# Moving the first gate's four tanh behind attention's last exponentials in a two-layer hybrid decoder

## The chip, the cores and the metric

The kernel runs on one core of one Trainium2 chip. The metric is the device time of one execution in microseconds (us). Five engines work side by side, each through its own list of instructions in order: TensorE (PE, with its weight loads as PEld), VectorE (DVE), ScalarE (ACT), GpSimd (POOL) and SyncE (SP), which here mostly issues loads. An instruction that needs another engine's result waits on a semaphore, and everything behind it on its engine waits too.

## The reference

The reference computes two layers on x of 512 tokens by 1024 features, in float32. Each layer does:

```
h = rmsnorm(x) ; z = h @ w_in       # q,k,v of attention, q,k,v,o,i,f of the mLSTM, gates g_a, g_m
att = sliding-window attention(q, k, v, sinks)      # 8 heads, 2 key heads, blocks of 128 queries
hm  = mLSTM in chunkwise form, per-head norm, times sigmoid(o)
mixed = sigmoid(g_a) * (att @ w_att_branch) + sigmoid(g_m) * (hm @ w_m_branch)
x = x + mixed @ w_out
x = x + relu(rmsnorm(x) @ w_ff1)^2 @ w_ff2
```

Attention's softmax is p = exp(s - m), divided by the sum of p and exp(sink - m). The sigmoid of a gate is computed as (1 + tanh(g / 2)) / 2. g_a and g_m have 1024 columns each, which the kernel works off in four groups of 512: gates 0 and 1 are g_a, gates 2 and 3 are g_m.

## The kernel before

Each float32 operand of a large product is split into a high and a low part in the reduced type fp32r, and a product is three matmuls into one PSUM buffer (high by high, high by low, low by high). The split of a weight chunk (`chunk`, L144 to L167) is one copy on ScalarE (`wh`, L166) and one subtraction on VectorE (`wl`, L167). Chunks come from memory through three landing buffers and are split into four pairs of `wh`, `wl`; a landing buffer is free for the next load when its `wl` is done.

`mixer` computes everything of a layer up to w_out. After the projections of attention's inputs, one long list of PE steps follows: the mLSTM's q and k (8 units of length), gate 0 (8), gate 1 (8), the first part of the mLSTM's v and o (2), and then the product of attention's output with w_att_branch. A unit of length is one chunk of 128 input features by 512 columns, 12 matmuls of 128x512. A gate's projection (`gate_steps`) gathers four PSUM buffers (`bank()`, five in all) over 8 chunks; then `ev` runs four times: VectorE multiplies each buffer by the norm's row into the tile `p` (L700) and so frees it, and at m == 3 ScalarE takes the tanh of all four tiles (L703).

Attention runs beside this list. `weave` takes the list and a second one, `side`, of (position, function) pairs, and calls each side function when the list has come to its position. There are 8 attention units, 4 query blocks by 2 key heads. Unit i's scores (`att_scores`, PE, then a copy on ScalarE, L604, and a masked copy on VectorE, L605) stand at 7 + 1.65 i, the softmax (`att_softmax`: maximum on VectorE, four exponentials L618 and one for the sink, L620, on ScalarE, division on VectorE) 1.25 later, the transposes of the probabilities on PE (`att_probs`, L52) and their split (L176, L177) 3.45 later, and the product with the values (`att_out`, PE, then L649 and L656 on ScalarE, L653 and L657 on VectorE) 5.65 later. Before each block, its queries and keys are transposed on PE and read out of PSUM by pairs of ScalarE and VectorE (`q_tr` L585 and L586, `k_tr` L563 to L566). All small products of attention (names `aux`) share three PSUM buffers.

What stands in an engine's list is decided when the kernel is built: a scheduler takes the calls in the order of `weave`, and orders each engine's instructions by the dependences, by its own estimates, and by priorities. `tc.high_priority()` lets an instruction go ahead of others that are ready, and `with tc.issue_after(i)` holds one back until instruction i has been placed. The evictions of a gate, `ev` with its tanh, run at high priority (`group_steps`, `finish`).

A ScalarE function needs its table loaded. The scheduler puts a table load ahead of the first function that the loaded table does not hold; attention's first exponentials run with the table that is loaded at the program's start (LN_EXP), and a load stands ahead of the first tanh of a layer.

The result of gate 0's tanh is read by VectorE in `a_steps(0, g0)`, after the product with w_att_branch, which begins at position 26 of the list.

Of the kernel before, what the change touches and what calls it, by code (L numbers as in the profile page):

```python
# [12 lines left out]
AF = mybir.ActivationFunctionType  # L13
# [20 lines left out]
def hybrid_kernel(ctx, tc, x, norm_mix, w_in, att_q_norm, att_k_norm, att_sinks, m_gate_bias,  # L34
# [3 lines left out]
    ve, sc, gp = nc.vector, nc.scalar, nc.gpsimd  # L38
# [34 lines left out]
    def slot(dt=F32, shape=(P, T)):  # L73
        return now["act"].tile(list(shape), dt, tag="a", name=nm("a"))
# [20 lines left out]
    def sm(shape, tag, bufs=None):  # L95
        return small.tile(list(shape), F32, tag=tag, name=nm(tag), bufs=bufs)
# [112 lines left out]
    def feat_steps(acts, srcs, evac):  # L209

        def mm(ps, c, w, a, first, last):
            mm3(ps, w[0][:, c], w[1][:, c], a[0], a[1], first, last)

        return group_steps(acts, srcs, evac, T, mm)
# [174 lines left out]
    def mixer(l, norm, late, order, phase):  # L389
# [9 lines left out]
        def wcols(c0, n):  # L399
            return lambda k: [W[k * P:(k + 1) * P, c0:c0 + n]]  # L400
# [150 lines left out]
        def k_vec(b):  # L551
            rope(kvi[:, b, 0:128].rearrange("p (h d) -> p h d", d=HD), b, HKV)

        def k_tr(b):

            ps = aux([P, P])
            pe.transpose(ps, kvi[:, b, 0:128], ident)
            for h in range(HKV):
                r = slice(64 * h, 64 * h + 64)
                o = slice(64 - 64 * h, 128 - 64 * h)  # L560
                c = slice((b + 1) * P, (b + 2) * P)
                g = gcols[1][r, l:l + 1]
                sc.activation(kTh[r, h, c], ps[r, :], AF.Copy, scale=g)  # L563
                sc.activation(kTh[o, h, c], ps[r, :], AF.Copy, scale=g)
                ve.scalar_tensor_tensor(kTl[r, h, c], ps[r, :], g, f32(kTh[r, h, c]), op0=ALU.mult, op1=ALU.subtract)
                ve.tensor_copy(kTl[o, h, c], f32(kTl[r, h, c]))  # L566

        def q_vec(b):
            rope(q_tok[b].rearrange("p (h d) -> p h d", d=HD), b, HQ)

        def q_tr(b):


            ps = aux()
            for j in range(4):
                pe.transpose(ps[:, j * P:(j + 1) * P], q_tok[b][:, j * P:(j + 1) * P], ident)
            for j in range(2):
                qT[b, j] = temp(F32R)
                t4 = qT[b, j].rearrange("p (i n t) -> p i n t", n=2, i=2)
                p4 = ps[:, 2 * j * P:2 * (j + 1) * P].rearrange("p (n t) -> p n t", n=2)  # L580
                for i in range(2):
                    r = slice(64 * i, 64 * i + 64)
                    o = slice(64 - 64 * i, 128 - 64 * i)
                    g = gcols[0][r, l:l + 1]
                    sc.activation(t4[r, i], p4[r], AF.Copy, scale=g)  # L585
                    ve.scalar_tensor_tensor(t4[o, i], p4[r], g, f32(t4[r, i]), op0=ALU.mult,  # L586
                                            op1=ALU.subtract)

        def att_scores(b, kv, hp):
# [14 lines left out]
                sc.activation(dst, p4[:, :, 0, :], AF.Copy)  # L604
            ve.copy_predicated(dst, tri_i.unsqueeze(1).to_broadcast([P, 2, P]), p4[:, :, 1, :])  # L605

        def att_softmax(b, kv):
            sp = sps[b, kv]
            s3 = sp.rearrange("p (h k) -> p h k", h=4)
            hs = slice(4 * kv, 4 * kv + 4)  # L610
            m = sm([P, 4], "m")
            ve.tensor_reduce(m, s3, axis=AX.X, op=ALU.max)
            ve.scalar_tensor_tensor(m, m, -1.0, nsinks[:, l, hs], op0=ALU.mult, op1=ALU.min)
            es = sm([P, 4], "es")
            ve.tensor_tensor(es, sinks[:, l, hs], m, op=ALU.add)
            den = sm([P, 4], "den")
            for i in range(4):
                sc.activation(s3[:, i, :], s3[:, i, :], AF.Exp, bias=m[:, i:i + 1],  # L618
                              accum_out=den[:, i:i + 1])
            sc.activation(es, es, AF.Exp)  # L620
            ve.tensor_tensor(den, den, es, op=ALU.add)
            ve.reciprocal(den, den)
            ve.tensor_tensor(s3, s3, den.unsqueeze(2).to_broadcast([P, 4, P]), op=ALU.mult)
# [69 lines left out]
        def gate_steps(g, last=False):  # L693


            sg = []

            def ev(m, ps):
                sg.append(wide[g][:, m, :] if g < 2 else slot())
                ve.tensor_tensor(sg[m], ps, row[0], op=ALU.mult)  # L700
                if m == 3:
                    for t in sg:
                        i = sc.activation(t, t, AF.Tanh, scale=0.5)  # L703
                    if last:
                        with tc.issue_after(i.ins):
                            sc.preload_act_table_set(LN_EXP)

            return sg, feat_steps(acts, wcols(C_G + 512 * g, 512), ev)
# [124 lines left out]
        def vo_steps(*ns):  # L833
# [4 lines left out]
        side = [(0, lambda: k_vec(0)), (0, lambda: q_vec(0)), (0, lambda: k_vec(1)), (0, lambda: q_vec(1)),  # L838
                (7 - 1.25, lambda: k_tr(0)), (7 - 1.75, lambda: q_tr(0))]
        for i, (b, kv) in enumerate(units):  # L840
            at = 7 + 1.65 * i
            side += [(at, lambda b=b, kv=kv: att_scores(b, kv, 0)),
                     (at + 1.25, lambda b=b, kv=kv: att_scores(b, kv, 1)),
                     (at + 1.25, lambda b=b, kv=kv: att_softmax(b, kv)),
                     (at + 3.45, lambda b=b, kv=kv: att_probs(b, kv)),
                     (at + 3.45 + 2.2, lambda b=b, kv=kv: att_out(b, kv))]
            if kv == 0 and b + 1 < NB:
                if b + 2 < NB:
                    side += [(at + 1, lambda b=b: k_vec(b + 2)), (at + 1, lambda b=b: q_vec(b + 2))]
                side += [(at + 2 * 1.65 - 1.75, lambda b=b: k_tr(b + 1)), (at + 2 * 1.65 - 2.15, lambda b=b: q_tr(b + 1))]  # L850
# [3 lines left out]
                                  (43.5, 1, 0), (45.0, 3, 0), (46.5, 1, 1), (48.0, 3, 1))]  # L854
        g0, s0 = gate_steps(0)
        g1, s1 = gate_steps(1)

        hm = q_tok
        hss = sm([P, NB, MH], "hss", 1)
# [129 lines left out]
        def sum_next(key, g):  # L989
            b = scratch["b"]  # L990
            with behind():
                ve.scalar_tensor_tensor(b, b, -1.0, wide[g][:, :, 0:H], op0=ALU.mult, op1=ALU.subtract)
            for p in range(2):
                of_chain(key, p)
# [34 lines left out]
        def ready_pair(n, p):  # L1029
            with behind():  # L1030
                h, lo = split(qa[0][:, 2 * p:2 * p + 2, :], get=boxed(n, 2 * p, 2))
            for k in range(2):
                wo[n, 2 * p + k] = h[:, k, :], lo[:, k, :]
            sum_a(p, 1, 1 if n == 5 else 0)

        def ready_w(n, k):
            raw = {3: qb, 7: qb, 2: qc}[n][k] if n in (3, 7, 2) else qa[0][:, k, :]
            if n == 2:
                get = boxed(n, k)
            elif n == 3:  # L1040
                get = lambda: temp(F32R)
            else:
                tags = iter(("wh", "wl"))

                def get():
                    t = next(tags)
                    return now["wsp"].tile([P, T], F32R, tag=t, name=nm(t))

            with behind():
                wo[n, k] = split(raw, get=get)  # L1050
            if n == 1 and k % 2:
                sum_a(k // 2, 0, 1)
            if n == 3:
                with tc.high_priority():
                    gp.dma_start(raw, of_out(0, 1, k)[:, 0, :], accum_op=ALU.add)
# [63 lines left out]
        for n in (1, 5, 6, 3, 7, 2):  # L1119
            fill += p_steps(n)  # L1120
        fill += p_steps(4, by_tokens)
        side = [(0.3, lambda: ready_w(1, 3)), (2.3, lambda: ready_pair(5, 0)), (4.3, lambda: ready_pair(5, 1)),
                (4.9, sum3), (6.2, lambda: ready_pair(6, 0)), (8.6, lambda: ready_pair(6, 1)),
                (10.3, lambda: sum_next("s2", 0)), (11.7, lambda: sum_next("s4", 1))]
# [505 lines left out]
    for l in range(DEPTH):  # L1630
        with start if l == 0 else ExitStack() as phase:
            if l > 0:
                psum_pools(phase, 3)
            norm = mixer(l, norm, late, order, phase)
        late = norm.steps(0, 1.5, 0.5)
        with ExitStack() as phase:
            psum_pools(phase, 2)
            norm = mlp(l, norm, late, phase)
        late = norm.steps(0, 1.5, 0.5, lambda k, norm=norm: turn_behind(norm, k)) if norm else []
        order = [4, 5, 6, 7, 0, 1, 2, 3]  # L1640
# [40 lines left out]
```

## Time and profile before

| what | us |
|---|---|
| median of 3 runs | 1277.46 (1277.41 to 1277.77) |
| the profiled execution, its own time | 1277.93 |
| its span, first to last instruction | 1276.2 |
| PE busy | 1266.2 (99%) |
| VectorE busy | 1040.0 (81%) |
| ScalarE busy | 793.1 (62%) |
| GpSimd busy | 256.4 (20%) |

Lines are given as L and a number; out<-in are the program's tile names: `mm` and `aux` are PSUM buffers, `i` the normed input, `t` and `a` working tiles, `p` the tiles of gates 0 and 1, `w` a landed weight chunk, `wh` and `wl` its split. A time in square brackets is idle time of the engine just before the instruction, with what ended it. PE's matmuls overlap, so that the durations of a row of them add up to more than the time that they take.

### The profile page before, as it was taken

How to read it: one execution, taken by the hardware profiler on the slowest of the kernel's cores; microseconds unless marked ns; L12 is line 12 of the kernel's file. 1: busy time of each engine (PE TensorE's matmuls, PEld its weight loads, DVE VectorE, ACT ScalarE, POOL GpSimd, SP SyncE). 2: the span in 40 equal slices, each digit the busy share in tenths (PEclk: the TensorE clock that was granted, in tenths of full speed). 3: DMA queues.
4: the chain of work that ended last, by engine and by line, in shares of the span. 5: the costliest groups of instructions: out<-in, count | busy, mean ns of one | idle time of the engine just before them, and what ended most of it. 6: DMA issues, size and time to landing. Idle time of an engine off the chain costs nothing.

```text
span 1276.2 us, 19228 instructions
## 1 busy us (share of the span) xinstructions
PE 1266.2 (99%) x6882; PEld 1089.0 (85%) x6882; DVE 1040.0 (81%) x1654; ACT 793.1 (62%) x1399; POOL 256.4 (20%) x337
## 2 busy tenths in 40 slices
PE   9999999999999999999999999999999999999998
PEld 7877888888889999999888778888888899999987
DVE  4689998688787887969947889876887879779697
ACT  5578578645656666656554875785455666565563
POOL 4503132021003031130114031310300120301210
PEclk9999999999999999999999999999999999999999
DMA  5426372466669798897224254635756697988953
GB/s 158 112 59 165 100 131 83 150 128 161 179 158 208 214 194 206 201 206 208 34 75 117 66 149 108 116 108 140 145 145 187 164 227 188 202 211 195 222 139 99
DMA packets 138927, 193.35 MB, mean 151 GB/s; under 512 B 10568, under 2 KB 79024, under 8 KB 138832
## 3 DMA queue, kind: packets, MB, share of 16 engines
q1 hardware_dynamic: 92992, 129.72, 33.2%
q0 software_dynamic: 45120, 62.00, 30.3%
q8 instruction: 54, 0.88, 0.3%
q10 hardware_dynamic: 720, 0.40, 0.1%
q14 instruction: 41, 0.34, 0.1%
HBM read 188.95 MB, written 2.10 MB: 150 GB/s over the span
## 4 chain that ended last, share of the span: by engine, by line
PE 91%; ACT 4%; DVE 3%; issue 1%; DMA 0%; ACTq 0%; DVEq 0%
PE mm L47 74%; PE aux L47 15%; PE aux L52 2%; ACT t L618 1%; DVE wl L167 1%; ACT wh L166 1%; ACT t L585 0%; DVE t L653 0%; ACT p L703 0%; DMA grow<-in_norm_mix_dram 0%; DVE t L586 0%; DMA w<-in_w_in_dram 0%; ACT t L176 0%; ACT L703 0%; DVE a L912 0%
## 5 line engine op out<-in xcount | busy, mean ns | idle before, releaser
L47 PE MATMUL mm<-i,wh 128*128 128x512 f32 (+1 forms) x1280 | 353.8, 363 | 0.0
L1162 ACT ACTIVATE wh<-raw 128x1024 fp32r<-128x1024 f32 x212 | 223.3, 1056 | 178.1 <-PE mm L47 99.8
L1163 DVE TENSOR_TENSOR wl<-raw,wh 128x1024 fp32r<-128x1024 f32 x212 | 256.0, 1224 | 80.5 <-ACT wh L1162 80.4
L47 PEld LDWEIGHTS mm<-i,wh 128*128 128x128 f32 x1280 | 223.2, 190 | 30.3
L47 PE MATMUL mm<-i,wl 128*128 128x512 f32 (+1 forms) x640 | 229.3, 359 | 0.0
L47 PE MATMUL mm<-wh,uh 128*128 128x512 f32 x440 | 172.0, 391 | 0.0
L47 PE MATMUL mm<-wl,uh 128*128 128x512 f32 x440 | 171.8, 391 | 0.0
L47 PE MATMUL mm<-wh,ul 128*128 128x512 f32 x440 | 171.4, 389 | 0.0
L1332 POOL DMA_DIRECT2D raw<-in_w_ff_dram x48 | 62.9, 1317 | 380.0 <-DMA raw<-in_w_ff_dram 241.0
L47 PEld LDWEIGHTS mm<-i,wl 128*128 128x128 f32 x640 | 121.0, 189 | 18.1
L167 DVE TENSOR_TENSOR wl<-w,wh 128x512 fp32r<-128x512 f32 (+1 forms) x144 | 97.3, 679 | 37.6 <-ACT wh L166 36.6
L166 ACT ACTIVATE wh<-w 128x512 fp32r<-128x512 f32 (+1 forms) x144 | 86.1, 603 | 62.7 <-PE mm L47 48.0
L47 PE MATMUL mm<-wh,i 128*128 128x512 f32 (+1 forms) x352 | 100.3, 359 | 0.6 <-ACT wh L166 0.6
L1217 DVE SCALAR_TENSOR_TENSOR x<-mm,ms,x 128x512 f32<-128x512 f32 x126 | 90.9, 747 | 8.5 <-PE mm L47 8.5
L47 PEld LDWEIGHTS mm<-wh,ul 128*128 128x128 f32 x440 | 82.6, 188 | 17.6
L47 PEld LDWEIGHTS mm<-wh,uh 128*128 128x128 f32 x440 | 82.8, 188 | 15.9
L47 PEld LDWEIGHTS mm<-wl,uh 128*128 128x128 f32 x440 | 82.8, 188 | 15.6
L1489 POOL DMA_DIRECT2D raw<-in_w_ff_dram x36 | 43.4, 1206 | 151.7 <-DVE wl L1163 100.9
L47 PEld LDWEIGHTS mm<-wh,i 128*128 128x128 f32 x352 | 62.0, 188 | 9.8 <-ACT wh L166 0.8
L47 PE MATMUL aux<-t,wh 128*128 128x256 f32 x384 | 69.5, 283 | 0.0
L47 PE MATMUL aux<-i,wh 128*128 128x256 f32 x384 | 69.5, 283 | 0.0
L47 PE MATMUL mm<-wl,i 128*128 128x512 f32 (+1 forms) x176 | 62.0, 352 | 0.0
(317 smaller groups left out, 2520.3 us busy)
## 6 DMA issues: line engine op xcount, KB each, us to landing
raw<-in_w_ff_dram SPq DMA_DIRECT2D x144, 512.0 KB, 4.9
raw<-in_w_ff_dram POOLq DMA_DIRECT2D x84, 512.0 KB, 7.8
w<-in_w_in_dram SPq DMA_DIRECT2D x112, 256.0 KB, 2.7
a<-in_w_in_dram POOLq DMA_DIRECT2D x32, 256.0 KB, 5.9
qa<-in_w_out_dram POOLq DMA_DIRECT2D x12, 512.0 KB, 6.0
a<-in_w_in_dram SPq DMA_DIRECT2D x16, 256.0 KB, 4.3
w<-in_w_att_branch_dram SPq DMA_DIRECT2D x16, 256.0 KB, 2.9
w<-in_w_m_branch_dram SPq DMA_DIRECT2D x16, 256.0 KB, 2.9
```

The source lines that it names most:

```text
L47: latest[0] = nc.tensor.matmul(*args, **kw)
L52: latest[0] = nc.tensor.transpose(*args)
L166: sc.activation(wh[:, :off], raw[:, :off], AF.Copy)
L167: ve.tensor_tensor(wl[:, :off], raw[:, :off], f32(wh[:, :off]), op=ALU.subtract)
L618: sc.activation(s3[:, i, :], s3[:, i, :], AF.Exp, bias=m[:, i:i + 1], accum_out=den[:, i:i + 1])
L1162: sc.activation(hi, src, AF.Copy)
L1163: ve.tensor_tensor(lo, src, f32(hi), op=ALU.subtract)
L1217: ve.scalar_tensor_tensor(xh[:, cc], ps[i][:, cc], ms[j][:, b:b + 1], xh[:, cc], op0=ALU.mult, op1=ALU.add)
L1332: gp.dma_start(to[h], src(h, i, j), accum_op=ALU.add)
L1489: gp.dma_start(to[h], src(h, i, j), accum_op=ALU.add)
```

## The change

The four tanh of gate 0 are no longer issued by `ev` when the gate's projection ends. `att_softmax` remembers its last instruction, the sink's exponential. Four side entries, at positions 22.6, 22.95, 23.3 and 23.65, each issue one tanh behind the sink's exponential of the unit whose softmax was called last. Unit 7's softmax stands at 7 + 1.65 * 7 + 1.25 = 19.8, so that is the last unit's. The tanh then have no raised priority. Gates 1 to 3 are as before.

```diff
+        last_exp = [None]
+
+        def late_tanh(t):
+            with tc.issue_after(last_exp[0].ins):
+                sc.activation(t, t, AF.Tanh, scale=0.5)
+
         def att_softmax(b, kv):
...
-            sc.activation(es, es, AF.Exp)
+            last_exp[0] = sc.activation(es, es, AF.Exp)
...
             def ev(m, ps):
                 sg.append(wide[g][:, m, :] if g < 2 else slot())
                 ve.tensor_tensor(sg[m], ps, row[0], op=ALU.mult)
-                if m == 3:
+                if m == 3 and g:
                     for t in sg:
                         i = sc.activation(t, t, AF.Tanh, scale=0.5)
...
+        side += [(22.6 + 0.35 * m, lambda m=m: late_tanh(g0[m])) for m in range(4)]
```

Numbers of lines behind the new helper are 6 higher in the changed kernel (L618 becomes L624), and 7 higher behind the new side entries. The order of SP's and GpSimd's instructions is the same in both. PE's, VectorE's and ScalarE's orders differ in layer 1 from the end of gate 0's projection to the start of the product with w_att_branch, and for ScalarE and VectorE in a second, smaller place behind it; layer 2 differs in the same way.

The first place is ScalarE where gate 0's projection has just ended, in the middle of attention. `p_642` is gate 0's tile, `t_1253` and `t_1258` are a block's transposed queries, `t_1197` is the score tile of the fifth unit, `es_1276` its sink. Before:

```order
L564 ACTIVATE kT_623<-aux_1296,gc_147 64x128
L703 ACT_TABLE_LOAD
L703 ACTIVATE p_642<-p_642 128x512 x4
L656 ACTIVATE a_638<-t_1237 128x128
L585 ACTIVATE t_1253<-aux_1248,gc_137 64x256
L563 ACTIVATE kT_623<-aux_1296,gc_147 64x128
L618 ACTIVATE t_1197,den_1278<-t_1197,m_1273 128x128 x2
L585 ACTIVATE t_1258<-aux_1248,gc_137 64x256
```

In ScalarE's changed order, from the same L564 on:

```order
L564 ACTIVATE kT_623<-aux_1296,gc_147 64x128
L662 ACTIVATE a_638<-t_1237 128x128
L166 ACTIVATE wh_1512<-w_1510 128x512
L585 ACTIVATE t_1253<-aux_1248,gc_137 64x256
L563 ACTIVATE kT_623<-aux_1296,gc_147 64x128
L564 ACTIVATE kT_623<-aux_1296,gc_147 64x128
L585 ACTIVATE t_1258<-aux_1248,gc_137 64x256
L604 ACTIVATE t_1306<-aux_1307 128x256
L166 ACTIVATE wh_1565<-w_1563 128x512
L585 ACTIVATE t_1258<-aux_1248,gc_137 64x256
L624 ACTIVATE t_1197,den_1278<-t_1197,m_1273 128x128 x4
L626 ACTIVATE es_1276<-es_1276 128x4
```

The load and the four tanh are gone from there; two weight splits and the last L585 now stand ahead of the exponentials.

The second place is PE a little later, in gate 1's projection (`wh_1411` before and `wh_1407` after are its second weight chunk, `wh_1456` before its third; `t_1114` holds the fourth unit's probabilities). Before:

```order
L47 MATMUL mm_1397<-i_115,wh_1411 128x512
L47 MATMUL mm_1397<-i_114,wl_1412 128x512
L47 MATMUL mm_1358<-i_114,wh_1456 128x512
L52 MATMUL aux_1317<-ident,t_1114 128x128 x4
L47 MATMUL aux_1336<-t_1210,v_111_625 128x512
```

PE in the changed order, around the same transposes:

```order
L47 MATMUL mm_1364<-i_114,wh_1407 128x512
L47 MATMUL mm_1364<-i_115,wh_1407 128x512
L47 MATMUL mm_1364<-i_114,wl_1408 128x512
L52 MATMUL aux_1317<-ident,t_1114 128x128 x4
L47 MATMUL aux_1336<-t_1210,v_111_625 128x512
```

The transposes and the product of the unit before stand behind the 13th matmul of the second and third chunk together before, and behind the 6th now.

The third place is the end of attention, on ScalarE. `es_1556` before and `es_1552` after are the last unit's sink, `t_1635` and `t_1631` the high part of its probabilities, `p_643` is gate 1's tile. Before:

```order
L620 ACTIVATE es_1556<-es_1556 128x4
L656 ACTIVATE a_636<-t_1604 128x128
L656 ACTIVATE a_638<-t_1604 128x128
L166 ACTIVATE wh_1734<-w_1732 128x512
L166 ACTIVATE wh_1749<-w_1747 128x512
L176 ACTIVATE t_1635<-aux_1630 128x512
L649 ACTIVATE t_1663<-aux_1658 64x512
L703 ACTIVATE p_643<-p_643 128x512 x2
```

ScalarE in the changed order:

```order
L626 ACTIVATE es_1552<-es_1552 128x4
L662 ACTIVATE a_636<-t_1600 128x128
L662 ACTIVATE a_638<-t_1600 128x128
L166 ACTIVATE wh_1734<-w_1732 128x512
L611 ACT_TABLE_LOAD
L611 ACTIVATE p_642<-p_642 128x512
L176 ACTIVATE t_1631<-aux_1626 128x512
L611 ACTIVATE p_642<-p_642 128x512 x2
L655 ACTIVATE t_1659<-aux_1654 64x512
L166 ACTIVATE wh_1749<-w_1747 128x512
L611 ACTIVATE p_642<-p_642 128x512
L709 ACTIVATE p_643<-p_643 128x512 x2
```

The load and the four tanh now stand here, the split of `wh_1749` behind three of them. On VectorE at the same place, before:

```order
L177 TENSOR_TENSOR t_1636<-aux_1630,t_1635 128x512
L167 TENSOR_TENSOR wl_1750<-w_1747,wh_1749 128x512
L700 TENSOR_TENSOR p_643<-mm_1358,t_477 128x512
L700 TENSOR_TENSOR p_643<-mm_1368,t_477 128x512
L700 TENSOR_TENSOR p_643<-mm_1393,t_477 128x512
L700 TENSOR_TENSOR p_643<-mm_1397,t_477 128x512
L653 TENSOR_TENSOR t_1664<-aux_1658,t_1663 64x256 x2
```

VectorE in the changed order:

```order
L177 TENSOR_TENSOR t_1632<-aux_1626,t_1631 128x512
L659 TENSOR_TENSOR t_1660<-aux_1654,t_1659 64x256
L706 TENSOR_TENSOR p_643<-mm_1354,t_477 128x512
L706 TENSOR_TENSOR p_643<-mm_1364,t_477 128x512
L706 TENSOR_TENSOR p_643<-mm_1389,t_477 128x512
L706 TENSOR_TENSOR p_643<-mm_1393,t_477 128x512
L167 TENSOR_TENSOR wl_1750<-w_1747,wh_1749 128x512
L659 TENSOR_TENSOR t_1660<-aux_1654,t_1659 64x256
```

The low part of the weight chunk has moved from ahead of gate 1's four evictions to behind them, and one half of an attention output's sum, which reads what ScalarE's L655 wrote, has moved ahead of them.

## The prediction

> **What bounds the kernel now.** I read the page first (shares by engine and the chain that ended last), then PE's instructions in order of time over the attention stretch of both layers, then ScalarE's and VectorE's over the same stretch.
>
> ```profile
> span 1276.2 us, 19228 instructions
> PE 1266.2 (99%) x6882; PEld 1089.0 (85%) x6882; DVE 1040.0 (81%) x1654; ACT 793.1 (62%) x1399; POOL 256.4 (20%) x337
> PE 91%; ACT 4%; DVE 3%; issue 1%; DMA 0%; ACTq 0%; DVEq 0%
> ```
>
> PE is busy for 99% of the span and carries 91% of the chain. Work that moves between rows of ScalarE is worth only what it takes from, or adds to, the moments in which PE's next matmul starts late. A busy PE hides part of these: a matmul is drawn 0.39 us long, while undisturbed ones start 0.23 us apart. So I take the distance between starts, not the idle time shown. PE in order of time, layer 1 (start, duration, instruction, count):
>
> ```profile
> 107.06 0.39 PE L47 MATMUL mm<-i,wh 128*128 128x512 f32 x1
> 107.51 0.66 PE L52 MATMUL aux<-ident,t 128*128 128x128 f32 x4
> 108.18 1.18 PE L47 MATMUL aux<-t,v 128*128 128x512 f32 x4
> ...
> 112.40 0.39 PE L47 MATMUL mm<-i,wl 128*128 128x512 f32 x1
> 113.02 1.17 PE L47 MATMUL aux<-t,v 128*128 128x512 f32 x4 [0.23 <-DVE t L653]
> ...
> 123.56 0.39 PE L47 MATMUL mm<-i,wl 128*128 128x512 f32 x1
> 124.12 0.63 PE L52 MATMUL aux<-ident,t 128*128 128x128 f32 x4 [0.17 <-ACT wh L166]
> 124.50 1.18 PE L47 MATMUL aux<-t,v 128*128 128x512 f32 x4
> ...
> 126.20 0.62 PE L47 MATMUL mm<-i,wh 128*128 128x512 f32 x2
> 126.66 0.39 PE L47 MATMUL mm<-i,wl 128*128 128x512 f32 x1
> ```
>
> 126.20 to 126.66 is two matmuls, so 0.23 us is the undisturbed step; 124.12 to 124.50 says that four transposes need 0.38. Against these the program loses 0.45 - 0.23 = 0.22 us at 107.06, 0.67 - 0.38 = 0.29 at 107.51, 0.62 - 0.23 = 0.39 at 112.40 and 0.56 - 0.23 = 0.33 at 123.56: 1.23 us. Layer 2 runs the same program 632.3 us later:
>
> ```profile
> 739.31 0.39 PE L47 MATMUL mm<-i,wh 128*128 128x512 f32 x1
> 739.79 0.66 PE L52 MATMUL aux<-ident,t 128*128 128x128 f32 x4
> 740.47 1.18 PE L47 MATMUL aux<-t,v 128*128 128x512 f32 x4
> ...
> 744.68 0.40 PE L47 MATMUL mm<-i,wl 128*128 128x512 f32 x1
> 745.30 1.17 PE L47 MATMUL aux<-t,v 128*128 128x512 f32 x4 [0.22 <-DVE t L653]
> ...
> 755.88 0.39 PE L47 MATMUL mm<-i,wl 128*128 128x512 f32 x1
> 756.40 0.63 PE L52 MATMUL aux<-ident,t 128*128 128x128 f32 x4
> ```
>
> 0.25 + 0.30 + 0.39 + 0.29 = 1.23 us again. These eight places, 2.46 us, are the large losses between the old place of the tanh and its new one, and the change cannot win much more than them.
>
> **The change part by part.** It adds and removes no instruction: 4 tanh per layer and the one table load ahead of them move, about 30 us to the right on ScalarE. No DMA moves; the rows of SP and POOL stand in the same order.
>
> *What leaves.* ScalarE in order of time at the old place:
>
> ```profile
> 99.46 0.36 ACT L564 ACTIVATE kT<-aux,gc 64x128 fp32r<-64x128 f32 x1
> 99.84 1.28 ACT L703 ACT_TABLE_LOAD   x1
> 101.13 2.19 ACT L703 ACTIVATE p<-p 128x512 f32<-128x512 f32 x4
> 103.23 0.29 ACT L656 ACTIVATE a<-t 128x128 fp32r<-128x128 f32 x1
> ...
> 106.47 0.47 ACT L585 ACTIVATE t<-aux,gc 64x256 fp32r<-64x256 f32 x1
> 106.96 0.21 ACT L620 ACTIVATE es<-es 128x4 f32<-128x4 f32 x1
> ```
>
> The block is 103.23 - 99.84 = 3.39 us (0.55 per tanh). Behind it wait three of the four L585 that read a block's transposed queries out of PSUM. The last of their VectorE partners (L586) ends at 106.97 + 0.49 = 107.46, and PE's transposes start at 107.51, in the PSUM buffer that this partner has just freed:
>
> ```profile
> 101.95 0.48 DVE L586 SCALAR_TENSOR_TENSOR t<-aux,gc,t 64x256 fp32r<-64x256 f32 x1
> ...
> 106.97 0.49 DVE L586 SCALAR_TENSOR_TENSOR t<-aux,gc,t 64x256 fp32r<-64x256 f32 x1 [0.79 <-ACT t L585]
> ...
> 100.74 0.40 PE L47 MATMUL mm<-i,wl 128*128 128x512 f32 x1
> ```
>
> So I take the first three losses (0.22 + 0.29 + 0.39 = 0.90, and 0.94 in layer 2) for the block's wake. With it gone I walked the new order with such durations. From 99.84: one split of an attention output (0.29) to 100.13; a weight split (0.6), as soon as PE is through with its buffer (row 100.74), to 101.5; L585 (0.47) behind its VectorE partner, which has one short instruction more ahead (101.95 + 0.1 + 0.48, say 102.6), to 103.1; L563 and L564 (0.36 each, 0.1 of wait) to 104.0; L585 to 104.4; a score copy and a weight split (0.4 and 0.5 from start to start) to 105.2. There the last L585 starts, not at 106.47, and its partner, behind a score mask, ends at 106.4. PE's new order has the same transposes 7 matmuls (1.6 us) earlier, at 105.7 in the walk. They now take the buffer of the key transposes, whose last reader ends at 105.5. So the three losses go.
>
> *What comes back.* ScalarE does not hand the 3.39 us to the softmax alone. Its new order puts two weight splits (wh, 0.6 each) ahead of the exponentials that follow; in my walk these end at 107.3 against 107.17 before. PE's attention rows also stand closer together. The walk leaves PE 0.1 to 0.3 us of slack at four waits between 105 and 113 and none at the last transposes (they want their scaled probabilities at 127.5, PE is there at 127.4). One such wait costs 0 when it is met, or 0.33 when it is not (123.56 above, a wait of this kind that the block does not cause). Bounds: 0 to 5 x 0.33 = 1.65 us a layer; I take 0.15, near the lower end, since the walk has four of the five met. The fourth loss of each layer (0.33 and 0.29) I leave as it is.
>
> *Where the block lands.* ScalarE at the end of attention:
>
> ```profile
> 127.96 0.19 ACT L620 ACTIVATE es<-es 128x4 f32<-128x4 f32 x1
> 128.06 0.49 ACT L656 ACTIVATE a<-t 128x128 fp32r<-128x128 f32 x2
> 128.46 0.62 ACT L166 ACTIVATE wh<-w 128x512 fp32r<-128x512 f32 x1
> 130.26 0.63 ACT L166 ACTIVATE wh<-w 128x512 fp32r<-128x512 f32 x1 [1.19 <-PE mm L47]
> 130.92 0.60 ACT L176 ACTIVATE t<-aux 128x512 fp32r<-128x512 f32 x1
> 131.69 0.60 ACT L649 ACTIVATE t<-aux 64x512 f32<-64x512 f32 x1 [0.17 <-PE aux L47]
> 133.48 1.23 ACT L703 ACTIVATE p<-p 128x512 f32<-128x512 f32 x2 [1.19 <-DVE p L700]
> ```
>
> Two idle pieces of 1.19 us are there to take it. On this clock: load 129.08 to 130.36, one tanh to 130.9, the last L176 at 130.9 as before; two tanh to 132.0, L649 (the low half of the next-to-last output) at 132.0 and not 131.69; the weight split of 130.26 now at 132.6, 2.3 us later; the fourth tanh to 133.7. Queued behind L649 on VectorE, newly, is one L653 and then the four evictions of the second gate's projection, which are also what PE's next PSUM buffer waits for:
>
> ```profile
> 132.76 2.55 DVE L700 TENSOR_TENSOR p<-mm,t 128x512 f32<-128x512 f32 x4
> 136.09 0.69 DVE L167 TENSOR_TENSOR wl<-w,wh 128x512 fp32r<-128x512 f32 x1
> ...
> 136.04 0.39 PE L47 MATMUL mm<-wh,i 128*128 128x512 f32 x1
> ...
> 138.31 0.39 PE L47 MATMUL mm<-wl,i 128*128 128x512 f32 x1
> ```
>
> L649 ends at 132.6, L653 (0.42) at 133.0, the first eviction (0.68) at 133.7; PE wants its buffer at 136.04: 2.3 us of slack. The four evictions end at 135.6, the delayed split's low part (0.69) at 136.3; PE wants it at 138.31: 2.0 us of slack. So the landing costs 0, covered by these slacks; if PE comes 0.75 us earlier and VectorE does not, 1.25 remain. If the cover were gone, at most the block less the slack would show, 3.39 - 2.0 = 1.4 us a layer.
>
> In the trace the first tanh starts 1.29 us after the load does (99.84 to 101.13). The Trainium skill (ScalarE: Activation LUTs, What ACT_TABLE_LOAD costs) adds a drain of about 1.38 us to a load of 1283 ns. The load agrees with the row, the drain is not in it. By the page the block would be an estimated 4.8 us, 2.0 - 1.38 leaves 0.6 us of slack at the landing, and the sum stays the same.
>
> A second, smaller reordering follows near 165 to 175 us (ScalarE's and VectorE's rows for the mLSTM maxima change places with weight splits). PE's rows there are unchanged and its own waits in the profile name none of those lines; I cost it at nothing.
>
> **The sum.** Layer 1: -0.90 + 0.15 = -0.75; layer 2: -0.94 + 0.15 = -0.79; together -1.5 us. The profiled execution took 1277.93 us (span 1276.2 and 1.7 around it), so it would be 1276.4. That execution lies 0.47 above the median of the runs shown, 1277.46; I give the time against the median: 1276.0.
>
> **The rivals.**
> - *Nothing is won.* The freed ScalarE time goes to weight splits that nobody waits for yet, the exponentials end no earlier (107.3 against 107.17), and PE, with its attention rows packed closer, waits about 0.9 us a layer in new places. For it: ScalarE's new order. Against it: the L585, not the exponentials, held PE at 107.51. Time: -1.84 + 1.84 = 0, so 1277.5.
> - *Slower.* VectorE stands still behind L649, which stands behind the load and three tanh, so the low part of the next weight chunk comes late and PE stops at 138.31 in each layer. It decides when that low part is more than 2.0 + 0.75 = 2.75 us late. At the bound, with the whole 3.39 us unhidden, two such stops and no relief: 2 x 1.4 = +2.8, so 1280.3. Against it: two idle pieces of 1.19 us on ScalarE.
> - *More than 0.2% faster.* All eight losses go and nothing comes back: -2.46, so 1275.0; to pass 0.2% some further loss outside this stretch must go too. Nothing in the profile ties one to ScalarE.
> - *The change does not do what it says.* Excluded: in the built order the load and the four tanh stand behind the last exponentials in both layers, and there are as many loads as before.
>
> **How the numbers follow.** What a measurement of this kernel can tell from no change is about 0.2%, 2.55 us. Chances: the forecast 0.62 (its own range 1275.0 to 1277.0), nothing won 0.20 (1277.0 to 1278.0), slower by some mechanism like the second rival 0.10 (1278 to 1281), faster than my bound 0.08. The range reaches from 1274.9, just past the removal of all eight losses, to 1278.3, a fifth of the slower rival's way. Within 0.2% lie the forecast, the first rival and a small part of the others, 0.82; beyond it 0.09 on either side.
>
> **What would show it.** Right: the losses in front of the transposes and attention outputs near 107 to 113 and 739 to 745 shrink to under 0.1 us; ScalarE shows load and tanh near 128 to 133; VectorE's four evictions run on time for PE, no PE wait near 136 to 138. Wrong: PE waits of 0.3 us or more in front of transposes between 105 and 128, or one behind a late low part near 138.

## The result, and the profile after

The changed kernel takes 1279.20 us (median of 20 runs, 1278.42 to 1280.45) against 1277.38 of the kernel before (20 runs, 1276.80 to 1277.92): a ratio of 1.0015, with a 95% interval of 1.0008 to 1.0021. It is 1.8 us slower; 1276.0 was forecast, with a range that ended at 1278.3. The profiled execution of the changed kernel took 1278.93 us, 1.0 more than that of before. Each of these two lies on the side of its median that is nearer to the other kernel, so what follows counts PE's time in single stretches of the program and not between the two ends.

The page of the changed kernel, span and busy shares, and the chain that ended last:

```profile
span 1277.2 us, 19230 instructions
PE 1267.3 (99%) x6882; PEld 1089.1 (85%) x6882; DVE 1044.3 (82%) x1654; ACT 794.1 (62%) x1399; POOL 256.6 (20%) x337
PE 92%; DVE 5%; ACT 1%; issue 1%; DMA 0%; DVEq 0%; POOL 0%; ACTq 0%; POOLq 0%
```

PE still fills the span, and VectorE has gone from 3% to 5% of the chain. PE in order of time, layer 1, where the prediction saw the losses at 107.06, 107.51, 112.40 and 123.56:

```profile
104.88 0.39 PE L47 MATMUL mm<-i,wl 128*128 128x512 f32 x1
105.53 0.63 PE L52 MATMUL aux<-ident,t 128*128 128x128 f32 x4 [0.27 <-DVE kT L565]
106.11 1.20 PE L47 MATMUL aux<-t,v 128*128 128x512 f32 x4
...
108.32 0.63 PE L47 MATMUL mm<-i,wh 128*128 128x512 f32 x2
109.33 0.74 PE L47 MATMUL aux<-kT,t 128*128 128x256 f32 x4 [0.38 <-DVE t L177]
...
116.08 0.40 PE L47 MATMUL mm<-i,wl 128*128 128x512 f32 x1
116.63 0.63 PE L52 MATMUL aux<-ident,t 128*128 128x128 f32 x4
```

The old losses are gone, all four of them, also that at 123.56, which the prediction had left as it is. With the undisturbed steps of the prediction (0.23 us a matmul, 0.38 for four transposes) the new ones are 0.65 - 0.23 = 0.42, 0.58 - 0.38 = 0.20, 1.01 - 0.46 = 0.55 and 0.55 - 0.23 = 0.32 us, 1.49 in place of 1.23. Smaller ones, 0.15 or less each and not listed, bring the difference over the stretch to 0.56. Layer 2 is alike:

```profile
738.61 0.39 PE L47 MATMUL mm<-i,wl 128*128 128x512 f32 x1
739.26 0.63 PE L52 MATMUL aux<-ident,t 128*128 128x128 f32 x4 [0.27 <-DVE kT L565]
739.85 1.20 PE L47 MATMUL aux<-t,v 128*128 128x512 f32 x4
...
742.05 0.62 PE L47 MATMUL mm<-i,wh 128*128 128x512 f32 x2
743.06 0.75 PE L47 MATMUL aux<-kT,t 128*128 128x256 f32 x4 [0.38 <-DVE t L177]
```

VectorE in that time, for the first two waits:

```profile
105.03 0.36 DVE L565 SCALAR_TENSOR_TENSOR kT<-aux,gc,kT 64x128 fp32r<-64x128 f32 x1
...
106.74 1.29 DVE L167 TENSOR_TENSOR wl<-w,wh 128x512 fp32r<-128x512 f32 x2
...
108.58 0.69 DVE L177 TENSOR_TENSOR t<-aux,t 128x512 fp32r<-128x512 f32 x1
```

L565 is the last reader of the key transposes' buffer, which PE's transposes at 105.53 take; L177 reads the buffer that the scores at 109.33 take, and stands behind the low parts of two weight chunks.

To compare kernels I measure PE's time over the whole stretch in which its order differs: from the last transpose of a key and value block, whose wait ends just ahead of the old place of the tanh, to the first matmul behind gate 1. Those two rows, for the kernel before:

```profile
98.75 0.30 PE L52 MATMUL aux<-ident,kvi 128*128 128x128 f32 x1 [0.44 <-DVE t L653]
...
134.42 0.39 PE L47 MATMUL mm<-wh,i 128*128 128x512 f32 x1
```

And for the changed kernel:

```profile
98.23 0.30 PE L52 MATMUL aux<-ident,kvi 128*128 128x128 f32 x1 [0.45 <-DVE t L659]
...
134.46 0.39 PE L47 MATMUL mm<-wh,i 128*128 128x512 f32 x1
```

That is 35.67 us before and 36.23 after; in layer 2 35.61 (731.03 to 766.64) and 36.23 (731.96 to 768.19). The stretch holds 0.56 + 0.62 = 1.18 of the 1.8 us.

Busy time of each engine (after the window and its length: PE, PEld, DVE, ACT, POOL) in the 19.5 us from 98.5, kernel before:

```profile
98.50:118.00 19.50, 18.95 (x92) 14.74 (x93) 17.25 (x44) 17.11 (x48) 6.94 (x8) 1.00 0.82 212
```

Changed kernel:

```profile
98.50:118.00 19.50, 18.70 (x93) 14.25 (x92) 18.95 (x47) 14.67 (x44) 6.59 (x8) 1.00 0.79 208
```

ScalarE has 2.4 us less to do there. VectorE, at 88% of the window before, is now at 97%. That by itself need not cost PE anything: in late_old_pe_tail, a kernel of the experiments below in which PE loses least, VectorE is at 94% of the same window:

```profile
98.50:118.00 19.50, 18.78 (x97) 15.60 (x98) 18.36 (x48) 14.16 (x44) 6.73 (x8) 1.00 0.79 212
```

The end of attention, ScalarE and then VectorE of the changed kernel:

```profile
128.12 1.28 ACT L611 ACT_TABLE_LOAD   x1
129.41 0.63 ACT L611 ACTIVATE p<-p 128x512 f32<-128x512 f32 x1
...
132.75 0.62 ACT L611 ACTIVATE p<-p 128x512 f32<-128x512 f32 x1
```

```profile
132.70 2.65 DVE L706 TENSOR_TENSOR p<-mm,t 128x512 f32<-128x512 f32 x4
135.27 0.68 DVE L167 TENSOR_TENSOR wl<-w,wh 128x512 fp32r<-128x512 f32 x1
```

The block landed where it was expected. VectorE's evictions end at 135.35 and the low part behind them at 135.95, while PE wants them at 136.09 and 138.36 and does not wait there. From the first matmul behind gate 1 (134.42 before, 134.46 here) to the next transposes on PE nothing has become longer. Those transposes, in the kernel before and then in the changed one:

```profile
168.07 0.41 PE L52 MATMUL aux<-ident,t 4*128 4x4 f32 x4
```

```profile
168.12 0.41 PE L52 MATMUL aux<-ident,t 4*128 4x4 f32 x4
```

That is 33.65 and 33.66 us.

### The profile page after: what moved, and what is told of

Read it like the earlier page. It is cut to its first block, busy times and chain, and to the rows that moved or that the text cites. A ratio compares the mean times of both kernels' runs of the same rounds, so it can differ in the third digit from the quotient of the medians.

```text
span 1277.2 us, 19230 instructions
## 1 busy us (share of the span) xinstructions
PE 1267.3 (99%) x6882; PEld 1089.1 (85%) x6882; DVE 1044.3 (82%) x1654; ACT 794.1 (62%) x1399; POOL 256.6 (20%) x337
## 4 chain that ended last, share of the span: by engine, by line
PE 92%; DVE 5%; ACT 1%; issue 1%; DMA 0%; DVEq 0%; POOL 0%; ACTq 0%; POOLq 0%
PE mm L47 75%; PE aux L47 15%; PE aux L52 2%; DVE wl L167 1%; DVE t L659 0%; DVE t L586 0%; DVE p L706 0%; DMA w<-in_w_in_dram 0%; ACT t L624 0%; DVE t L605 0%; DVE t L629 0%; ACT t L585 0%; ACT wh L166 0%; DVE t L177 0%; DVE a L663 0%
```

## The experiments

Three theories fit this profile. Theory A in the expectations: the new order of PE costs the time, because its attention rows stand 7 matmuls earlier than ScalarE and VectorE can serve them. Theory B: the block costs it where it lands. Theory C: VectorE's and ScalarE's new order in the second place (150 to 180 us) costs it.

To part these, an engine's order had to be held while something else changes. For that a kernel notes the instructions of an engine as they are issued, and then chains those of one place in a given order by edges that carry no semaphore. They bind the scheduler alone (cuts are marked by dots):

```
+        fixed = [...]          # places 508 to 649 of PE's list, in the order of before
+        fixed = [pes[n + 3387 * l].ins for n in fixed]
+        for first, then in zip(fixed, fixed[1:]):
+            tc.add_manual_dep(then, first.name, mybir.DependencyInfo(
+                mybir.DependencyClass.NoSync, mybir.DependencyReason.DATA), reason="order of PE")
```

That is late_old_pe, made from the changed kernel; early_new_pe is the kernel before with PE's instructions chained in the order of the changed one. The same is done for ScalarE and VectorE (`sc.log`, `ve.log`) where a text says that they are held. In kernels that hold these two, all their rows name one line, L50, so that rows are told by their tiles.

All results together. S is PE's stretch defined above, in layers 1 and 2 of the profiled execution:

| kernel | tanh of gate 0 | PE's order | S, us | median, us | ratio to before (95%) |
|---|---|---|---|---|---|
| before | early | old | 35.67 / 35.61 | 1277.38 | |
| changed | late | new | 36.23 / 36.23 | 1279.20 | 1.0015 (1.0008 to 1.0021) |
| late_old_pe | late | old | 34.85 / 34.84 | 1276.72 | 1.0000 (0.9991 to 1.0009) |
| early_new_pe | early | new | 37.42 / 37.88 | 1281.31 | 1.0030 (1.0019 to 1.0042) |
| no_tanh0 | none | new | 36.24 / 36.24 | 1280.04 | 1.0020 (1.0011 to 1.0029) |
| tanh0_twice | both | old | 35.69 / 35.68 | 1278.72 | 1.0010 (1.0001 to 1.0019) |
| late_old_tail | late | new | 36.23 / 36.32 | 1278.98 | 1.0012 (1.0003 to 1.0021) |
| early_new_tail | early | old | 35.62 / 35.68 | 1277.55 | 1.0002 (0.9993 to 1.0011) |
| late_old_pe_tail | late | old | 34.82 / 34.83 | 1275.77 | 0.9988 (0.9979 to 0.9996) |
| late_l177_first | late | new | 36.01 / 36.02 | 1278.83 | 1.0009 (1.0000 to 1.0018) |
| no_low_parts | late | new | 35.81 / 35.17 | 1276.81 | 0.9995 (0.9987 to 1.0004) |
| early_load_moved | early, load at 51 | old | 34.89 / 34.97 | 1275.37 | 0.9984 (0.9975 to 0.9992) |
| no_tanh0_old_tail | none | new | 36.24 / 36.26 | 1278.96 | 1.0012 (1.0003 to 1.0021) |
| tanh0_twice_old_tail | both | old | 35.62 / 35.66 | 1277.51 | 1.0001 (0.9991 to 1.0010) |

The times of the kernel before in the later runs, to which the ratios refer, were 1277.41, 1277.47 and 1277.49. A ratio takes in all runs, not the median alone: late_old_pe, whose runs reach from 1275.71 to 1281.36, has a ratio of 1.0000 with a median 0.7 lower. S comes from one execution of each kernel, but kernels with the same order of PE and the block in the same place agree in it within 0.1 us, where nothing else in the stretch was changed (35.61 to 35.69 for early and old, 36.23 to 36.32 for late or none and new, 34.82 to 34.85 for late and old).

### The two causes apart: where the tanh stand, and PE's order

> The changed kernel, but PE's instructions of the attention stretch are held by order-only edges in exactly the order of before, in both layers; the four tanh and the load stay late, ScalarE and VectorE are ordered by the scheduler. Theory A (PE's new order is what costs: its attention rows come 7 matmuls earlier than ScalarE and VectorE can serve them): the changed kernel's PE losses of 0.42, 0.20, 0.56 and 0.32 us near 105, 108 and 116 go, and so do the old ones near 107 and 112, since ScalarE is free; the stretch from the key and value transposes of unit 5 to gate 1's end becomes at least 0.6 us a layer shorter than in the changed kernel; 1276.3 to 1277.9 us in all, the rest depending on the second place near 178 us (0 or 0.45). Theory B (the load and the tanh at the landing cost it): as long as the changed kernel, 1279.2 within 0.5.

> The kernel before, tanh and load at their old place, but PE held by order-only edges in exactly the order of the changed kernel. Theory A: PE's rows now come early and ScalarE's block is there too, so PE waits longer than in either kernel, at least 0.6 us a layer over before, 1278.6 to 1281. Theory B: 1277.4 within 0.5, because nothing lands late.

Measured: 1276.72 us, and 1281.31, which is 0.3 over the upper end of what was expected. With the old order the late tanh shorten S to 34.85 and 34.84, 0.82 and 0.77 under the kernel before. PE at the place of the old losses, in late_old_pe_tail (further below, where S is the same and the runs lie closer together):

```profile
107.12 0.40 PE L66 MATMUL mm<-i,wh 128*128 128x512 f32 x1
107.35 0.60 PE L72 MATMUL aux<-ident,t 128*128 128x128 f32 x4
107.71 1.17 PE L66 MATMUL aux<-t,v 128*128 128x512 f32 x4
...
110.36 0.63 PE L66 MATMUL aux<-kT,t 128*128 128x256 f32 x4
111.46 0.63 PE L72 MATMUL aux<-ident,t 128*128 128x128 f32 x4 [0.47 <-DVE t L50]
```

0.23 and 0.36 from start to start: the transposes that lost 0.22 and 0.29 lose nothing. The fourth loss is gone too, with PE in the same order as before:

```profile
122.98 0.40 PE L66 MATMUL mm<-i,wl 128*128 128x512 f32 x1
123.22 0.60 PE L72 MATMUL aux<-ident,t 128*128 128x128 f32 x4
```

0.24 from start to start, where the kernel before took 0.56. So this loss hung on the block as well. In its place there is a new wait of 0.47 ahead of the transposes at 111.46, which costs 1.10 - 0.47 = 0.63 us (four matmuls of scores take 0.47 when undisturbed, 114.70 to 115.17 in the kernel before), and one of 0.24 ahead of the scores at 103.15. With the new order and the block at its old place, PE in early_new_pe:

```profile
105.24 0.40 PE L48 MATMUL mm<-i,wl 128*128 128x512 f32 x1
107.41 0.66 PE L54 MATMUL aux<-ident,t 128*128 128x128 f32 x4 [1.77 <-DVE t L589]
```

The transposes come to the head of PE's queue at 105.5 and stand there until 107.41, the time at which VectorE had served them before too. All matmuls behind them wait along. Theory A holds in both directions, and theory B falls with the first run: the block is late in late_old_pe, and S is the shorter for it. In the totals late_old_pe cannot be told from the kernel before (1.0000); it is S that shows its gain, and late_old_pe_tail the total.

### Whether the landing costs anything

> Gate 0's four tanh are left out altogether (its gate is then not a sigmoid); PE's order is exactly that of the changed kernel, ScalarE's up to the last exponentials too, and the table load stands ahead of gate 1's tanh. Theory A: the same losses as in the changed kernel near 105, 108 and 116 us (0.42, 0.20, 0.56, 0.32), so 1278.5 to 1279.5 although the tanh cost nothing anywhere. Theory B: without a landing 1277.4 or less.

> Gate 0's four tanh with the load at the old place, and four more of them at the new place (gate 0 gets the tanh of its tanh); PE's order is exactly that of the kernel before. Theory A: the attention stretch is that of before (losses 0.22, 0.29, 0.39, 0.33), the four more tanh (2.2 us on ScalarE) are hidden, 1277.4 within 0.5. Theory B: the landing shows, at least 0.5 us a layer, 1278.4 or more.

The edits to the changed kernel, the first line for no_tanh0 and the others for tanh0_twice. The first kernel leaves gate 0's tanh out, the second takes them twice:

```
-        side += [(22.6 + 0.35 * m, lambda m=m: late_tanh(g0[m])) for m in range(4)]
...
-                if m == 3 and g:
+                if m == 3:
```

S is 36.24 without any tanh of gate 0, as in the changed kernel to 0.01 us, and 35.69 and 35.68 with eight of them, as before. The totals (1280.04 and 1278.72) miss what theory A said, by 0.5 and by 0.8 us; that of tanh0_twice lies on B's side. Another place is behind it: the scheduler had ordered 150 to 180 us anew in both. The profiled execution of tanh0_twice was the longest of its 11, 1280.61 us, and shows it best. PE lost there

```profile
173.27 0.39 PE L47 MATMUL mm<-wh,i 128*128 128x512 f32 x1
174.41 0.49 PE L47 MATMUL mm<-wh,i 128*128 128x512 f32 x1 [0.75 <-ACT wh L166]
175.14 0.50 PE L47 MATMUL mm<-wl,i 128*128 128x512 f32 x1 [0.23 <-DVE wl L167]
```

0.91 + 0.50 us behind a weight chunk that came late: SyncE issued its load at 168.46 and not at 167.09, since on VectorE an instruction of 1.21 us (L777) stood ahead of the low part that frees its landing buffer. The profiled execution of no_tanh0 was the shortest of its 11 (1278.77) and shows no loss of this size, so its longer median is put down to this place by the next run alone. Two more runs have the second place held as in the kernel before:

> As no_tanh0 (gate 0's four tanh left out, PE's order that of the changed kernel), with the second place held in the order of before. If the landing of the block costs nothing, this is as long as late_old_tail, which has the block: a stretch of 36.2 us and 1279.0 within 0.4. Theory B (the landing costs): 1278.2 or less.

> As tanh0_twice (four tanh at the old place, four more at the new; PE's order that of before), with the second place held in the order of before, so that its loss of 1.4 us near 174 us goes. Theory A: a stretch of 35.7 us and 1277.4 within 0.4, since four late tanh without a load are hidden. Theory B: 1278.0 or more.

Measured 1278.96, against 1278.98 of late_old_tail, which has the block; and 1277.51, against 1277.49 of the kernel before in those runs. The landing of the four tanh costs nothing that these runs can tell. They do not take the load away: without the tanh it stands ahead of gate 1's, at 133.82 us. But PE's time from gate 1's end to the transposes that stand at 168.07 in the kernel before settles both: it is 33.65 us, within 0.01, in both layers of all 14 kernels, with load and tanh landing there, with one of them, or with neither (the kernel before, and early_load_moved below). And ahead of gate 1's end S has the losses listed above, none of them behind 117 us in the changed kernel larger than 0.1.

### The second place by itself

> The changed kernel; only the second place (ScalarE and VectorE from some 150 to 180 us in each layer) is held by order-only edges in the order of before. PE's order and attention's rows are those of the changed kernel. Theory C (VectorE's new order there delays the low part that PE waits for at 178.66 in layer 1): that loss of 0.33 us goes, PE between gate 1's end and 212 us is 0.45 us faster in layer 1 and the same in layer 2; 1278.3 to 1279.0 in all. Rival (that wait comes from when a load lands, not from the order): 1279.2 within 0.2.

> The kernel before with its tanh where they were; only the second place is held in the order of the changed kernel. Theory C: a PE wait of 0.3 us or more near 178 us in layer 1 and none in layer 2; 1277.6 to 1278.1. Rival: 1277.4 within 0.2.

The edit chains places 205 to 244 of ScalarE's list and 280 to 320 of VectorE's in each layer, in late_old_tail in the order of before, in early_new_tail (made from the kernel before) in that of the changed kernel:

```
+        fixed = [sc.log[n + 628 * l].ins for n in fixed]
...
+        fixed = [ve.log[n + 825 * l].ins for n in fixed]
```

In the changed kernel PE waited there once, in layer 1:

```profile
177.88 0.61 PE L47 MATMUL mm<-wh,t 128*128 128x512 f32 x2
178.66 0.50 PE L47 MATMUL mm<-wl,t 128*128 128x512 f32 x1 [0.16 <-DVE wl L734]
```

With the old order of the second place this wait is gone, and the median is 1278.98, 0.2 under 1279.20, a difference within the spread of the runs. The new order put into the kernel before causes no such wait, and its median is 0.1 us higher (1277.55 against 1277.47), also within the spread. So theory C explains at most some tenths of a microsecond, and not by the order alone.

### Both orders held: what ScalarE's freed time is worth

> Tanh late, PE held in the order of before in the attention stretch, and the second place held in the order of before. Theory A with C: what is left is what ScalarE's freed 3.39 us give, 0.8 us a layer; 1275.4 to 1276.2, under late_old_pe's 1276.72. Rival (the gain of late_old_pe came from its own reordering behind attention): 1276.7 or more.

The edits of late_old_pe and late_old_tail together. Measured: 1275.77 us, a ratio of 0.9988 (0.9979 to 0.9996). This is near the forecast of 1276.0, but it is reached by the change together with two orders that it does not keep by itself, and by other terms: four old losses went and not three, and more came back. The runs also lie closer together than those of late_old_pe (1275.57 to 1276.93, against 1275.71 to 1281.36).

### Why the new order waits

> The changed kernel with all three engines held in its own order; on VectorE alone, in each layer, one weight chunk's low part (L167, 0.6 us) moves from ahead of the low part of a unit's probabilities (L177) to behind the next division (L629). Theory A says that PE's 0.56 us near 108.32 is a wait for the PSUM buffer that this L177 frees: it falls under 0.2 us in both layers, and the time to 1278.3 to 1278.9. Rival (something else is as late there, the next wait takes its place): 1279.2 within 0.2.

The edit, in VectorE's chain, where 206 and 218 are the low parts of two weight chunks, 172 the L177, and 165 the division (all other rows of the three engines as in the changed kernel):

```
-  206, 218, 163, 172, 164, 182, 165
+  206, 163, 172, 164, 182, 165, 218
```

The loss near 109 went (109.29 behind 108.83, two matmuls), and another came 2.4 us later:

```profile
109.29 0.63 PE L66 MATMUL aux<-kT,t 128*128 128x256 f32 x4
...
110.81 0.48 PE L66 MATMUL mm<-i,wl 128*128 128x512 f32 x1
111.69 1.17 PE L66 MATMUL aux<-t,v 128*128 128x512 f32 x4 [0.40 <-DVE t L50]
```

0.88 - 0.23 = 0.65 us in place of 0.55 + 0.14. S fell by 0.22, the median by 0.4, into theory A's range. Both were right in part: the wait for this L177 is gone in both layers (in layer 2 the 1.01 us from 742.05 to 743.06 became 0.46), and most of it came back at the next wait, as the rival said.

> The changed kernel with all engines held in its own order; VectorE's low parts (L167, 0.6 us each) of gate 1's first seven weight chunks are left out in both layers, and PE multiplies by the high part in their place (as many matmuls; gate 1's result is less exact). Theory A2 (in the changed order VectorE, 97% busy from 98.5 to 118 us against 88% before, is what PE's attention rows wait for): PE's stretch from the last transposes at 98.2 to the first matmul behind gate 1 falls from 36.23 to 35.3 us or less in both layers, the time to 1277.5 or less. Rival (the waits are the length of one chain of scores, softmax and split, however free VectorE is): 36.0 or more, 1278.8 or more.

```
+                if bare[0]:            # gate 1's first seven chunks
+                    ve.log.append(None)
+                    return wh, wh
                 ve.tensor_tensor(wl[:, :off], raw[:, :off], f32(wh[:, :off]), op=ALU.subtract)
```

1276.81 us, 2.4 under the changed kernel (PE multiplies by `wh` where `wl` stood, so the result is less exact). S fell to 35.17 in layer 2 but only to 35.81 in layer 1, so the expectation for S was met in one layer of two. VectorE's busy time in the same window:

```profile
98.50:118.00 19.50, 18.72 (x95) 14.68 (x94) 17.14 (x44) 14.75 (x45) 7.17 (x9) 1.00 0.80 211
```

17.14 us, less than the kernel before had. One wait stays:

```profile
103.73 1.07 PE L66 MATMUL mm<-i,wh 128*128 128x512 f32 x4
105.08 0.63 PE L72 MATMUL aux<-ident,t 128*128 128x128 f32 x4 [0.27 <-DVE kT L50]
105.66 1.20 PE L66 MATMUL aux<-t,v 128*128 128x512 f32 x4
```

1.35 for four matmuls (0.91) is 0.44, and 0.58 - 0.38 is 0.20: the first loss of the changed kernel stands as it was. The loss near 108 is gone in both layers. What parts the layers is one wait: in layer 1 the transposes at 110.17 wait 0.51 us for VectorE (0.69 lost), in layer 2 the same row at 741.93 does not wait. They read what the division before them wrote, and this one instruction took twice as long in layer 1. Layer 1, then layer 2:

```profile
108.33 1.69 DVE L50 TENSOR_TENSOR t<-t,den 128x512 f32<-128x512 f32 x1
```

```profile
740.76 0.81 DVE L50 TENSOR_TENSOR t<-t,den 128x512 f32<-128x512 f32 x1
```

Both overlap in time with two instructions of GpSimd on tiles of the same shape, which took 2.60 us together in layer 1 and 1.89 in layer 2, against 0.64 us each when they stand alone (111.94 and 113.25); that the two engines held each other up is not shown by a run.

So the new order's losses are of two kinds. That at 105 is a wait for one reading of a PSUM buffer, which PE's row comes ahead of; this run says little of what would relieve it, since none of the low parts left out stands on VectorE between 99 and 106 us in the changed kernel. The later ones go or move when VectorE is relieved.

### The load alone

> The kernel before with its tanh at their old place, but the table load issued behind the last logarithm near 51 us, where ScalarE idles 1.2 us; PE's attention stretch and the second place are held in the order of before. The block at 99.84 is then 2.1 and not 3.39 us. Theory A: the three L585 behind it come 1.28 us earlier, PE's losses of 0.22 and 0.29 at 107 go in both layers and that of 0.39 at 112 in part: a stretch of 35.0 to 35.2 us, 1276.0 to 1276.8. Rival (the load is hidden and the tanh alone delay the L585): 35.6 and 1277.4.

```
-            sc.activation(fl, fw, AF.Ln)
+            ln = sc.activation(fl, fw, AF.Ln)
+            with tc.issue_after(ln.ins):
+                nc.scalar.preload_act_table_set('exp_and_others')
```

Measured: 1275.37 us, 0.9984 (0.9975 to 0.9992), the fastest of all, and faster than the expectation's range of 1276.0 to 1276.8. S is 34.89 and 34.97, as short as with all the tanh away to 0.13 us; it holds 0.78 + 0.64 = 1.42 of the 2.1 us, and where the rest was gained was not followed. The load lies in ScalarE's idle time:

```profile
50.80 0.22 ACT L50 ACTIVATE fl<-fw 128x16 f32<-128x16 f32 x1 [0.24 <-DVE fw L50]
51.04 1.28 ACT L470 ACT_TABLE_LOAD   x1
52.33 1.15 ACT L50 ACTIVATE wh<-w 128x512 fp32r<-128x512 f32 x2
```

And at the old place the first of the three L585 starts at 102.30, not at 103.55 as in the kernel before, and the last at 104.81, not at 106.47:

```profile
102.30 0.47 ACT L50 ACTIVATE t<-aux,gc 64x256 fp32r<-64x256 f32 x1
...
104.81 0.47 ACT L50 ACTIVATE t<-aux,gc 64x256 fp32r<-64x256 f32 x1
```

Of the 3.39 us of the block, the 1.29 of the load were enough to cost PE what it lost; the tanh can stay where they were. This needs PE's old order held as well: when the load is moved and nothing held, the scheduler builds exactly the changed kernel's order of PE. That version was not run.

## Why the prediction was wrong, point by point

- *The block's wake* (0.90 and 0.94 us): the three losses go, as forecast, once PE's order is held. The fourth (0.33 and 0.29), which the prediction took for one that the block does not cause, goes too. What comes back in that order is 0.63 + 0.24 in layer 1, so that S gains 0.82 and 0.77 a layer. That these lie near the forecast's 0.75 and 0.79 is in part luck: a gain that was left out and a cost that was taken too small partly cancel. Whether it was the L585 alone and not the exponentials is not shown, since in early_load_moved and in the changed kernel both come earlier.
- *What comes back* (0.15 a layer): this step failed, and with it the forecast. Against the old order with the same late block, the new order of PE cost 36.23 - 34.85 = 1.38 us in layer 1 and 36.23 - 34.84 = 1.39 in layer 2, nine times as much and near the upper bound of 1.65 that the prediction gave. Its own sign of being wrong, waits of 0.3 us or more in front of transposes between 105 and 128, came true at 105.53 and 116.63 (0.42 and 0.32 lost). The walk let PE's transposes come 7 matmuls earlier and took that for harmless, with 0.1 to 0.3 us of slack at four waits. In its clock, in which this stretch begins 0.52 us later (98.75 against 98.23), PE was there at 104.88 + 0.23 + 0.52 = 105.6 as walked, but the last reader of the key transposes' buffer ended at 105.39 + 0.52 = 105.9, not 105.5. At the next wait VectorE had two weight low parts ahead of L177, and 0.55 us were lost. An error of 0.4 us in a walk of six microseconds was larger than the slacks that it found.
- *The price of a missed wait* (0.33): the losses measured 0.62, 0.55 and 0.32. Where one row waits for a buffer that a whole chain frees, the size of the wait is the error of the order, as the 1.94 us of early_new_pe show.
- *The landing* (0): right. PE's time behind gate 1's end is the same 33.65 us in every kernel, whether the block lands there or not.
- *The second place* (0): nearly. It cost the profiled execution 0.49 us in layer 1 (77.57 against 77.08 from gate 1's end to the `aux<-a,a` rows at 211.50 and 212.03), and held in the old order it is worth 0.2 of the median. Some 0.2 to 0.4 us of the 1.8 stay unexplained: in late_old_tail 1278.98 less 1277.47 is 1.51, of which S holds 0.56 + 0.71 = 1.27.
- *The rivals.* The first (nothing won, PE waits anew in new places) had the mechanism, and sized it at 0.9 us a layer where it is 1.4; with that size it is slower than before, which the forecast gave to another mechanism, VectorE behind L649. The second (VectorE stuck behind L649) did not happen: no wait stands near 136 to 138. The upper end of the range, 1278.3, lies three tenths of the way from 1277.46 to this rival's 1280.3, not a fifth as the prediction says.
- *The table load.* 128.12 to 129.41 and 51.04 to 52.33 are 1.29 us from the load to the next instruction, as at 99.84. The drain that the Trainium skill adds (ScalarE: Activation LUTs, What ACT_TABLE_LOAD costs) is not seen at these places either.

## What to carry to other kernels

Where a scheduler sets the order, a moved instruction is two changes: its own time, and the new order of engines that it does not run on. Price the second by itself, by holding the order of the bottleneck engine; here it was worth 1.4 us a layer against 0.8 for the first. An earlier place in the queue of an engine that is 99% busy is no gain but a risk: nothing behind it can start if its operands are 0.4 us late, so a slack that is smaller than the error of the estimate counts as none. And a busy share does not tell which it is: VectorE was at 97% of the window where PE lost 1.4 us and at 94% where it did not.

## What the runs showed that was not expected

- Moving 1.29 us of table load out of a block of 3.39 us gave nearly the whole gain of moving all of it (S of 34.89 and 34.97, against 34.85 and 34.84), at the better median, 1275.37 against 1275.77.
- Order matters tens of microseconds away: four more tanh at 128 to 133 us left PE's order and S alone, yet through the scheduler they cost 1.7 us of PE's time near 174 us in the profiled executions, that of the new order being the longest of its 11 (77.11 us from gate 1's end to the `aux<-a,a` row near 212 with the old order, 78.83 with the new; the medians differ by 1.2, 1278.72 against 1277.51).
- The spread of a kernel's runs depends on the order as well: late_old_pe ranged from 1275.71 to 1281.36 us, and with the second place held from 1275.57 to 1276.93. What differs between its executions was not seen, since only one of them was profiled; that a weight chunk's landing decides it is a guess from the wait at 174.41.
